# Six small tiles placed ahead of the token operands xH and xL: a shift of 224 bytes per partition

## The chip, the cores and the metric

The kernel runs on one core of a Trainium2 chip. The metric is the device time of one execution in microseconds (us); the time of a kernel is the median of its runs. One execution was also recorded by the hardware profiler, and all rows below come from that one. Each core has a matrix engine (TensorE, PE in the rows; PEld is its loading of weights), a vector engine (VectorE, DVE), a scalar engine (ScalarE, ACT), GpSimd (POOL) and a queue engine (SyncE, SP). They share a memory of 128 partitions, SBUF; an address below is a byte offset inside a partition.

## The reference: what is computed

One transformer block over 256 tokens of width 2048: an attention and recurrence mixer, and then a product-key expert layer (PEER) with 16,384 experts.

```
mod = silu(c) @ ada_w + ada_b                 # six rows of 2048: sh1, sc1, gt1, sh2, sc2, gt2
h = rms_norm(x, norm_mix_g) * (1 + sc1) + sh1
x = x + gt1 * hybrid_mixer(h, w_in, w_out, ...)     # z = h @ w_in, attention, RG-LRU, y @ w_out
h = rms_norm(x, norm_ffn_g) * (1 + sc2) + sh2
q = h @ peer_wq                               # 256 x 2048, scored against 16 sets of 128 keys
...                                           # top 16 of each half, top 16 of their sums, softmax g
act = gelu(einsum('td,thkd->thk', h, down[e])) * g
x = x + gt2 * einsum('thk,thkd->td', act, up[e])
```

The kernel computes the down product for all 16,384 experts (`h @ down.T`), multiplies by a dense table of gates that is zero for experts not picked, and multiplies by all of `up`.

## The kernel before, in words

Weights stream from HBM in tiles `raw` of 1 MB (`load`, L177), four buffers deep, on SyncE's queue. `next_part` (L273) takes half of such a tile and splits it: ScalarE rounds it to the type float32r (`wh`, L197), VectorE subtracts to get the remainder (`wl`, L198). Activations are split in the same way: `xH` and `xL` hold the 256 tokens of the current product input, 16 slices of 128 features by 256 tokens; `ah` and `al` hold the activations of the experts. Each product is then the sum of three matmuls: high by high, high by low, low by high.

There are two forms of it, and they differ in which operand is loaded into the array (stationary, 128 columns) and which is streamed through it (moving):

- `mm_sub` (L350, matmuls at L346 to L348): tokens are stationary, 128 at a time; weights move, 512 columns at a time. It is used with `xH` and `xL` for the input projection (results `f`, `a`, `r`, `xg`) and the output projection (`y`), and with `ah` and `al` for the up product (`u`).
- `mm_turn` (L356, matmuls at L363 to L365): weights are stationary, 128 columns at a time; tokens move, all 256 at once. It is used for the queries (`wq`) and the down product (`d`), both with `xH` and `xL`.

In `mm_turn` the two operands of a matmul are `wh[:, kk, ws]` (stationary) and `bH[:, kc]` (moving), where `bH` is `xH`:

```
T.matmul(o, wh[:, kk, ws], bH[:, kc], start=f and i % 2 == 0, stop=False)
T.matmul(o, wh[:, kk, ws], bL[:, kc], start=False, stop=False)
T.matmul(o, wl[:, kk, ws], bH[:, kc], start=False, stop=e and i % 2 == 1)
```

The gate logits (`gl`) use the same three products with 24 columns of weights stationary and the tokens moving.

The order of the program is: adaLN rows and the input projection (0 to 205 us), attention and recurrence with the rest of the projection between them (to 364 us), the output projection (to 474 us), the queries (to 574 us), the first 14 of 32 blocks of the down product with the building of the gate table (`w`) between their matmuls (to 930 us), and then blocks of the up product and the other blocks of the down product in turn, to the end. The order on every engine is fixed when the program is built.

Tiles of the pool `cp` live through the whole kernel and get their addresses in the order in which the code asks for them. In the built program they begin at byte 16,512 with `con`, `sm`, `row`, `cb`, `mod`, `cs` (32,512 to 32,576), then `xH`, `xL`, and then six small tiles for the decay of the recurrence (`spl`, `nsp`, `hb`, `e8`, `s8`, `q8`, 224 bytes together), which `softplus` (L417) fills at the start and `recurrence` (L734) reads.

Of the kernel before, what the change touches and what calls it, by code (L numbers as in the profile page):

```python
# [7 lines left out]
F32 = mybir.dt.float32  # L8
# [7 lines left out]
P = 128  # L16
# [8 lines left out]
RB = 8  # L25
# [40 lines left out]
def kernel(  # L66
# [26 lines left out]
    cp = ctx.enter_context(tc.tile_pool(name="cp", bufs=1))  # L93
# [19 lines left out]
    cb = cp.tile([P, D], F32, name="cb")  # L113
    mod = cp.tile([P, 6, NDC], F32, name="mod")
    cs = cp.tile([P, NDC], F32, name="cs")
    xH = cp.tile([P, NDC, S], F32R, name="xH")
    xL = cp.tile([P, NDC, S], F32R, name="xL")
    ident = con[:, C_ID:C_ID + P]
# [291 lines left out]
            yield  # L410
            A.copy(dst[:, j * 512:(j + 1) * 512], bp)

    spl = cp.tile([P, RB], F32, name="spl")
    nsp = cp.tile([P, RB], F32, name="nsp")
    hb = cp.tile([P, 2, RB], F32, name="hb")

    def softplus():  # L417
        e8 = cp.tile([P, RB], F32, name="e8")
        s8 = cp.tile([P, RB], F32, name="s8")
        q8 = cp.tile([P, RB], F32, name="q8")  # L420
        lam = sm[:, S_LAM:S_LAM + 8]
        A.activation(e8, lam, AF.Abs)
        A.activation(e8, e8, AF.Exp, scale=-1.0)
        V.tensor_scalar(s8, e8, 2.0, None, OP.add)
        V.reciprocal(s8, s8)
        V.tensor_mul(s8, s8, e8)
        V.tensor_mul(q8, s8, s8)
        V.tensor_scalar(spl, q8, 1.0 / 17, 1.0 / 15, OP.mult, OP.add)
        for kk in (13, 11, 9, 7, 5, 3, 1):
            V.tensor_mul(spl, spl, q8)  # L430
            V.tensor_scalar(spl, spl, 1.0 / kk, None, OP.add)
        V.tensor_mul(spl, spl, s8)
        V.tensor_scalar(q8, lam, -1.0, 0.0, OP.mult, OP.max)
        V.scalar_tensor_tensor(out=spl, in0=spl, scalar=2.0, in1=q8, op0=OP.mult, op1=OP.add)
        V.tensor_scalar(nsp, spl, -4.0, None, OP.mult)
        V.tensor_scalar(spl, spl, 2.0, None, OP.mult)
        V.tensor_scalar(hb, sm[:, S_BA:S_BA + 16].rearrange("p (a k) -> p a k", a=2), 0.5, None, OP.mult)
# [33 lines left out]
    for q in range(4):  # L471
        V.tensor_tensor(xt[:, 4 * q:4 * q + 4], xt[:, 4 * q:4 * q + 4], rr.unsqueeze(1).to_broadcast([P, 4, S]), OP.mult)

    softplus()

    def wide(name):
# [938 lines left out]
```

## Time and profile before

| | |
|---|---|
| median of 3 runs | 2073.27 us (2071.88 to 2073.3) |
| the profiled execution | 2070.29 us, its span 2068.5 us |
| PE busy | 1998.7 us, 97% of the span, 12602 matmuls |
| PEld busy | 1769.3 us, 86% |
| DVE busy | 1451.6 us, 70% |
| ACT busy | 1018.0 us, 49% |
| mean granted clock of TensorE | 0.987 of full speed |
| HBM traffic | 245 GB/s over the span |

Busy time of PE is the union of the times in which a matmul is in the array. Matmuls overlap: a matmul of `d` lasts 282 ns in the record, but the next one starts long before it ends. The pace of PE is therefore the distance from one start to the next, which a listing in order of time shows, and not the duration.

### The profile page before, as it was taken

The page shows a single profiled execution, that of the slowest core. Times are in us where ns is not written, and L with a number is a line of the kernel's source. Part 1 is how long each engine was busy: PE and PEld are TensorE (multiplying, and loading weights), DVE is VectorE, ACT ScalarE, POOL GpSimd, SP SyncE. Part 2 cuts the span into 40 slices and gives each one's busy share as a digit, 9 for nine tenths or more (in the row PEclk, how much of TensorE's full clock was granted, in tenths as well). Part 3 has the DMA queues.
Part 4 walks back from the last instruction along what each step waited for, and adds up shares of the span by engine and source line. Part 5 has one row for each costly group of instructions (what it writes and reads, how often), then busy time and mean ns, then how long its engine had stood idle before and what let it go on. Part 6 is the DMA issues. An engine that isn't in the chain of part 4 may idle for free.

```text
span 2068.5 us, 31265 instructions
## 1 busy us (share of the span) xinstructions
PE 1998.7 (97%) x12602; PEld 1769.3 (86%) x12602; DVE 1451.6 (70%) x2149; ACT 1018.0 (49%) x1454; POOL 61.0 (3%) x95
## 2 busy tenths in 40 slices
PE   5999997998999999999999999999999999999998
PEld 4777665778999999998888789999999999999997
DVE  7888999987999666546667766665555555555566
ACT  3445676545447887644444434444444444444442
POOL 0000000000000000001000000000000000000000
PEclk8999998998999999999999999999999999999999
DMA  9897788994555656768777877775566666565563
GB/s 374 331 371 314 265 336 319 347 344 173 174 182 185 246 207 241 278 242 296 255 242 254 285 248 259 255 262 197 194 199 207 204 203 206 195 205 201 196 223 132
DMA packets 75873, 509.12 MB, mean 246 GB/s; under 512 B 8528, under 2 KB 9040, under 8 KB 20176
## 3 DMA queue, kind: packets, MB, share of 16 engines
q1 hardware_dynamic: 63792, 450.50, 60.5%
q0 software_dynamic: 11936, 56.63, 8.2%
q8 instruction: 98, 1.61, 0.3%
q14 instruction: 47, 0.39, 0.1%
HBM read 478.78 MB, written 28.31 MB: 245 GB/s over the span
## 4 chain that ended last, share of the span: by engine, by line
PE 75%; issue 10%; DVE 9%; DMA 4%; ACT 1%; POOL 1%; DVEq 0%; SPq 0%; POOLq 0%; ACTq 0%
PE d L363 10%; PE d L365 10%; PE d L364 10%; PE u L347 7%; PE u L348 7%; PE u L346 7%; PE w L1198 3%; DVE wl L198 3%; DVE av L219 2%; DMA raw<-in_ada_w_dram 2%; PE wq L363 2%; PE wq L364 2%; PE wq L365 1%; PE a L347 1%; PE a L348 1%
## 5 line engine op out<-in xcount | busy, mean ns | idle before, releaser
L198 DVE TENSOR_TENSOR wl<-raw,wh 128x1024 fp32r<-128x1024 f32 x649 | 789.7, 1222 | 475.9 <-ACT wh L197 475.1
L197 ACT CAST wh<-raw 128x1024 fp32r<-128x1024 f32 x649 | 679.6, 1050 | 826.7 <-PE u L348 372.2
L363 PE MATMUL d<-xH,wh 128*128 128x256 f32 x2048 | 577.7, 282 | 0.0
L364 PE MATMUL d<-xL,wh 128*128 128x256 f32 x2048 | 573.0, 280 | 0.0
L365 PE MATMUL d<-xH,wl 128*128 128x256 f32 x2048 | 572.2, 279 | 0.3 <-DVE wl L198 0.3
L347 PE MATMUL u<-wl,ah 128*128 128x512 f32 x1024 | 399.4, 390 | 3.4 <-DVE wl L198 3.3
L346 PE MATMUL u<-wh,ah 128*128 128x512 f32 x1024 | 398.6, 389 | 0.0
L348 PE MATMUL u<-wh,al 128*128 128x512 f32 x1024 | 398.5, 389 | 0.0
L364 PEld LDWEIGHTS d<-xL,wh 128*128 128x128 f32 x2048 | 385.4, 188 | 0.7
L363 PEld LDWEIGHTS d<-xH,wh 128*128 128x128 f32 x2048 | 385.1, 188 | 0.7
L365 PEld LDWEIGHTS d<-xH,wl 128*128 128x128 f32 x2048 | 385.1, 188 | 0.5 <-DVE wl L198 0.5
L347 PEld LDWEIGHTS u<-wl,ah 128*128 128x128 f32 x1024 | 192.2, 188 | 44.9 <-DVE wl L198 5.9
L348 PEld LDWEIGHTS u<-wh,al 128*128 128x128 f32 x1024 | 192.3, 188 | 40.0
L346 PEld LDWEIGHTS u<-wh,ah 128*128 128x128 f32 x1024 | 192.3, 188 | 39.6
L219 DVE SCALAR_TENSOR_TENSOR av<-av,cb 128x2048 f32<-128x2048 f32 x64 | 145.9, 2285 | 5.3 <-DMA av<-in_ada_w_dram 5.3
L1182 DVE TENSOR_TENSOR oh<-con,idT 128x1024 f32<-128x1024 f32 x64 | 78.0, 1224 | 62.5 <-PE w L1198 62.5
L1203 ACT ACTIVATE oh<-oh,gT 128x128 f32<-128x128 f32 x256 | 83.3, 396 | 26.3 <-DVE oh L1182 26.1
L363 PE MATMUL wq<-xH,wh 128*128 128x256 f32 x256 | 73.2, 287 | 2.5 <-ACT xH L197 2.5
L364 PE MATMUL wq<-xL,wh 128*128 128x256 f32 x256 | 72.9, 285 | 0.0
L365 PE MATMUL wq<-xH,wl 128*128 128x256 f32 x256 | 72.5, 283 | 0.0
L1259 DVE TENSOR_TENSOR acc<-acc,u 128x512 f32<-128x512 f32 x112 | 71.6, 681 | 0.0
L1198 PE MATMUL w<-oh 128*128 128x128 f32 x512 | 69.8, 276 | 0.0
(359 smaller groups left out, 2008.3 us busy)
## 6 DMA issues: line engine op xcount, KB each, us to landing
raw<-in_down_dram SPq DMA_DIRECT2D x128, 1024.0 KB, 5.2
raw<-in_up_dram SPq DMA_DIRECT2D x128, 1024.0 KB, 5.1
av<-in_ada_w_dram SPq DMA_DIRECT2D x64, 1024.0 KB, 7.0
raw<-in_w_a_dram SPq DMA_DIRECT2D x32, 1024.0 KB, 9.1
raw<-in_ada_p_dram SPq DMA_DIRECT2D x16, 1024.0 KB, 7.3
raw<-in_w_out_dram SPq DMA_DIRECT2D x16, 1024.0 KB, 8.0
raw<-in_wq_dram SPq DMA_DIRECT2D x16, 1024.0 KB, 5.5
wd<-stg POOLq DMA_DIRECT2D x8, 2048.0 KB, 8.0
```

What stands on the lines that cost most here:

```text
L197: A.copy(dst_h, src)
L198: V.tensor_tensor(dst_l, src, dst_h.bitcast(F32), OP.subtract)
L219: V.scalar_tensor_tensor(out=t, in0=t, scalar=1.0, in1=cb, op0=OP.mult, op1=OP.mult, accum_out=m)
L346: T.matmul(o, ah, bh, start=first, stop=False)
L347: T.matmul(o, ah, bl, start=False, stop=False)
L348: T.matmul(o, al, bh, start=False, stop=last)
L363: T.matmul(o, wh[:, kk, ws], bH[:, kc], start=f and i % 2 == 0, stop=False)
L364: T.matmul(o, wh[:, kk, ws], bL[:, kc], start=False, stop=False)
L365: T.matmul(o, wl[:, kk, ws], bH[:, kc], start=False, stop=e and i % 2 == 1)
L1182: V.tensor_tensor(oh, iota.unsqueeze(1).unsqueeze(1).to_broadcast([P, 4, 2, P]), idT[:, 4 * q:4 * q + 4].unsqueeze(3).to_broadcast([P, 4, ...
L1198: T.matmul(wps[p_][:, k * P:(k + 1) * P], oh[:, k, 1], oh[:, k, 0], start=True, stop=True)
L1203: A.activation(ohs[p_][:, k, 0], ohs[p_][:, k, 0], AF.Copy, scale=gT[:, t:t + 1])
```

## The change

The six small tiles are allocated right after `cs`, ahead of `xH` and `xL`, instead of after them. They take 224 bytes, so `xH` and `xL` stand 224 bytes higher, and the small tiles 32,768 bytes lower. The pool ends at the same byte, so no other tile moves. The instructions of every engine, their order and what they wait for are the same in both programs; only addresses differ.

```diff
     mod = cp.tile([P, 6, NDC], F32, name="mod")
     cs = cp.tile([P, NDC], F32, name="cs")
+
+    spl = cp.tile([P, RB], F32, name="spl")
+    nsp = cp.tile([P, RB], F32, name="nsp")
+    hb = cp.tile([P, 2, RB], F32, name="hb")
+    e8 = cp.tile([P, RB], F32, name="e8")
+    s8 = cp.tile([P, RB], F32, name="s8")
+    q8 = cp.tile([P, RB], F32, name="q8")
     xH = cp.tile([P, NDC, S], F32R, name="xH")
     xL = cp.tile([P, NDC, S], F32R, name="xL")
...
-    spl = cp.tile([P, RB], F32, name="spl")
-    nsp = cp.tile([P, RB], F32, name="nsp")
-    hb = cp.tile([P, 2, RB], F32, name="hb")
-
     def softplus():
-        e8 = cp.tile([P, RB], F32, name="e8")
-        s8 = cp.tile([P, RB], F32, name="s8")
-        q8 = cp.tile([P, RB], F32, name="q8")
```

The addresses of the matmul operands in the two built programs. Slices of these tiles start at multiples of 512 bytes from the tile's start, so the remainders hold for every slice of 128, 256 or 512 columns:

| tile | before | after | rest by 512, before and after | rest by 64 |
|---|---|---|---|---|
| `xH` | 32,576 | 32,800 | 320, 32 | 0, 32 |
| `xL` | 48,960 | 49,184 | 320, 32 | 0, 32 |
| `wh`, `wl` (pool `wp`, 3 buffers each) | 98,336 to 118,816 | the same | 32 | 32 |
| `wh`, `wl` (pool `xp`, first stage alone) | | the same | 96 | 32 |
| `ah`, `al` (4 buffers each) | from 161,824 | the same | 32 | 32 |

Against the weights `wh` and `wl` of the pool `wp`, the token operands of the input, output, query and down products thus stand 288 bytes off (by 512) before, and 0 after. Those of the up product, `ah` and `al`, stand 0 off in both.

## Rows read from the trace of the kernel before

**Rows 1.** Busy time by stretch: us, each engine's busy us (instructions), granted clock, DMA.
```profile
core 0: us, PE busy (x) PEld busy (x) DVE busy (x) ACT busy (x) POOL busy (x), PEclk, DMA share, GB/s
0.00:205.00 205.00, 175.58 (x722) 138.55 (x723) 168.96 (x217) 92.01 (x137) 0.99 (x6) 0.95 0.89 350
205.00:364.00 159.00, 139.25 (x832) 92.27 (x830) 151.16 (x367) 105.56 (x243) 2.61 (x4) 0.95 0.79 301
364.00:474.00 110.00, 102.58 (x468) 82.34 (x468) 96.73 (x133) 53.64 (x77) 4.58 (x9) 0.95 0.90 342
474.00:574.00 100.00, 99.44 (x825) 99.04 (x825) 88.11 (x358) 48.09 (x60) 0.54 (x1) 0.97 0.49 169
574.00:930.00 356.00, 352.84 (x3005) 351.27 (x3005) 244.94 (x326) 236.92 (x461) 14.62 (x26) 1.00 0.64 226
930.00:1210.00 280.00, 277.09 (x1318) 231.68 (x1317) 198.08 (x230) 121.69 (x120) 20.26 (x28) 1.00 0.77 267
1210.00:2000.00 790.00, 789.48 (x5166) 722.76 (x5166) 460.19 (x473) 337.08 (x343) 16.32 (x20) 1.00 0.63 214
```

**Rows 2.** What PE waited for: us in total, times, longest us.
```profile
PE f L346 <- ACT xH L197: 15.4, 1, 15.4
...
PE u L347 <- DVE wl L198: 3.3, 4, 1.6
...
PE d L365 <- DVE wl L198: 0.3, 1, 0.3
```

**Rows 3.** Groups by line: form, count, busy us, mean ns, idle before.
```profile
L363 PE MATMUL d<-xH,wh 128*128 128x256 f32 x2048 | 577.7, 282 | 0.0
...
L363 PEld LDWEIGHTS d<-xH,wh 128*128 128x128 f32 x2048 | 385.1, 188 | 0.7
...
L363 PE MATMUL wq<-xH,wh 128*128 128x256 f32 x256 | 73.2, 287 | 2.5 <-ACT xH L197 2.5
...
L346 PE MATMUL y<-wh,xH 128*128 128x512 f32 x128 | 51.7, 406 | 3.6 <-ACT xH L197 3.6
...
L346 PE MATMUL a<-wh,xH 128*128 128x512 f32 x128 | 49.3, 397 | 1.8 <-ACT wh L197 1.8
...
L346 PE MATMUL f<-wh,xH 128*128 128x512 f32 x96 | 37.9, 415 | 15.4 <-ACT xH L197 15.4
...
L346 PE MATMUL xg<-wh,xH 128*128 128x512 f32 x32 | 13.5, 428 | 0.0
...
L346 PE MATMUL r<-wh,xH 128*128 128x512 f32 x32 | 12.9, 413 | 1.7 <-ACT wh L197 1.7
```

**Rows 4.** PE in order of time, a block of `d`: start us, us, what.
```profile
1221.34 0.28 PE L363 MATMUL d<-xH,wh 128*128 128x256 f32 x1
...
1243.74 0.39 PE L346 MATMUL u<-wh,ah 128*128 128x512 f32 x1
```

**Rows 5.** PE in order of time, the output projection.
```profile
437.83 0.40 PE L347 MATMUL y<-wl,xH 128*128 128x512 f32 x1
...
442.50 0.40 PE L346 MATMUL y<-wh,xH 128*128 128x512 f32 x1
```

**Rows 6.** PE in order of time, a block of the up product.
```profile
1289.99 0.39 PE L346 MATMUL u<-wh,ah 128*128 128x512 f32 x1
...
1299.96 0.39 PE L348 MATMUL u<-wh,al 128*128 128x512 f32 x1
```

**Rows 7.** PE in order of time, the gate logits.
```profile
262.77 0.28 PE L346 MATMUL gl<-xH,wh 128*24 128x256 f32 x1
...
264.36 0.28 PE L348 MATMUL gl<-xH,wl 128*24 128x256 f32 x1
```

**Rows 8.** Weight loads in order of time, merged: 8 loads before matmuls of one column.
```profile
354.88 0.97 PEld L879 LDWEIGHTS nha<-con,sqa 128*128 128x128 f32 x8
```

**Rows 9.** Groups by line: the casts that write `wh` and `xH`, and the subtractions.
```profile
L197 ACT CAST wh<-raw 128x1024 fp32r<-128x1024 f32 x648 | 679.1, 1051 | 826.7 <-PE u L348 372.2 <-PE d L364 297.3 <-PE y L348 44.2
...
L197 ACT CAST xH<-x1T 128x512 fp32r<-128x512 f32 x8 | 4.6, 615 | 0.8 <-DVE x1T L1060 0.7
```

## The prediction

> **What bounds the kernel now.** I read the busy times by stretch first, then what PE waited for, then the pace of its matmuls in the listing in order of time. In the stretches from 574 us on PE is busy 352.8 of 356, 277.1 of 280 and 789.5 of 790 us, at full clock; VectorE has 58 to 71% and the DMA engines 63 to 77% [rows 1]. The listed waits of PE for VectorE come to 3.3 us in `u` and 0.3 us in `d` [rows 2]. So from the queries (474 us) on, the end is set by how fast one matmul follows another, and the other engines have room. Before 474 us it is different: the DMA engines are busy 79 to 90% of the time and VectorE 82 to 95%, with PE at 86 to 93% [rows 1]. There, a faster matmul would mostly wait.
>
> The reader should then look at paces, not durations. A block of `d` has 192 matmuls (8 steps, 2 slices, 4 column groups, 3 products); the first starts at 1221.34 us and the first matmul behind the block at 1243.74 [rows 4]. That is 22.40 / 192 = 116.7 ns for 256 columns. Counted at one column per cycle of the full 2.4 GHz, 256 columns would take 106.7 ns, so 10.0 ns are lost, or 0.039 ns per column. In `y`, 20 matmuls lie between 437.83 and 442.50 [rows 5]: 233.5 ns for 512 columns, which need 213.3; 20 ns are lost, again 0.039 per column. In `u`, 44 matmuls lie between 1289.99 and 1299.96 [rows 6]: 226.6 ns, 13.3 lost, 0.026 per column.
>
> `y` and `u` run the same form: the same moving tiles `wh` and `wl`, 512 columns, stationary tiles of 128 by 128. What differs is the stationary tile: `xH` and `xL` at a remainder of 320 (by 512), 288 away from that of the weights, against `ah` and `al`, which have the weights' own remainder of 32. `d` has the roles exchanged, the same distance of 288, and the same loss per column as `y`. The gate logits move the same `xH` with only 24 columns of weights to load: 14 matmuls between 262.77 and 264.36 [rows 7], 113.6 ns for 256 columns, 0.027 per column. So moving `xH` itself can go at the better pace, and it is in company with a full weight load at another remainder that it goes at the worse one.
>
> **The change part by part.** It adds and removes no instruction, wait or DMA. Three things move.
>
> The small tiles (32 or 64 bytes per partition) get other addresses. They are read as scalars and filled once; I take 0.
>
> Writes to `xH` and `xL` land at another remainder. A cast of 512 columns into `xH` takes 615 ns at the old place, and one of 1024 columns into `wh`, which already has the new remainder, 1051 ns [rows 9]. Half of the latter is less than the former, and a start-up time explains it, so I take 0. If the whole difference, 2 x 615 - 1051 = 179 ns, came from the remainder, the 24 casts would give back at most 4 us, in stages that PE alone does not bound.
>
> The matmuls that read `xH` and `xL` get both operands at the same remainder. Their number: `d` has 3 x 2048 = 6144 and `wq` 3 x 256 = 768 [rows 3], 6912 together, in stretches that PE bounds. `y` has 3 x 128, `a` 3 x 128, `f` 3 x 96, `xg` and `r` 3 x 32 each: 1248, all before 474 us.
>
> No row has a moving operand of 256 float32r columns at remainder 32 beside a full weight load at 32. The nearest are `u` (all remainders 32, but 512 columns) and `gl` (256 columns moving, but a short load). Both lose 0.026 to 0.027 ns per column. With 0.026, `d` comes to 106.7 + 6.7 = 113.4 ns, 3.3 ns less than now. A floor lies just below: loads of 128 columns of weights that nothing else slows follow each other at 0.111 us (8 loads in 0.97 us, of which one, 188 ns, is the last one's own length [rows 3, 8]: (970 - 188) / 7). So the most that `d` could gain is 116.7 - 111.7 = 5.0 ns, and the least is nothing or a loss (below). I take 3.3, since `u` and `gl` agree from two sides: 6912 x 3.3 = 22.8 us.
>
> For `y` and its like the analogue is complete (`u`, all operands then at the same remainders): 233.5 - 226.6 = 6.9 ns, 1248 x 6.9 = 8.6 us if all of it counted. In their stretches DMA and VectorE stand close behind, so I count a third, 3 us; the bounds are 0 and 8.6.
>
> What takes over when PE goes faster: at 3% more pace VectorE rises from 88 to 91% in the queries, and from 69 to 71% in the first blocks of `d`; nothing becomes the bound there.
>
> The sum on the profiled execution's own time is 2070.3 - 22.8 - 3 = 2044.5 us. It lies 3.0 us under the median of the runs, so I forecast 2073.3 - 25.8 = 2047.5, and give 2047.
>
> One rule speaks against all this. Row for row, `y` and `u` differ by 6.9 ns with the same moving tile [rows 5, 6], and nothing but the stationary tile's place differs. The Trainium skill ("SBUF — State Buffer", section "Who interferes with whom") says that PE has two independent read ports, one for the moving operand and one for the weight load, and never waits on anyone. By that rule no address could matter and the sum would be 0, a time of 2073. The trace does not agree with it as far as `y` is concerned, unless another cause stands behind those 6.9 ns; that is the first rival.
>
> **The rivals.** *No effect.* `y` could be slow for a reason that the change leaves as it is: that `xH` lies low in the partition (32 to 65 KB) and `ah` at 161 KB or more, or that the projection stages have more DMA traffic (0.79 to 0.90 against 0.63 [rows 1]). Against traffic: the pace in `u` hardly varies, and `d` at 0.63 loses as much per column as `y`. Against the place: `d` moves `xH` slowly and `gl` moves the same `xH` fast. Time: 2073, give or take 4. The Trainium skill's rule on the ports, cited above, would put it here. Chance 0.12.
>
> *The stationary operand's own remainder is what counts.* Then `xH` at a multiple of 64 was bad as a stationary operand, only `y` and its like gain, and `d`, whose weights stay where they are, keeps its 116.7 ns. Time: 2073.3 less 0 to 8.6, about 2070 at the third counted above. For it: it fits `y` against `u`. Against it: the equal loss per column in `d` would be chance. Chance 0.08.
>
> *The loss goes with the weight load, and grows when both streams start at the same place.* This is the other side. A load lasts about as long as 256 columns move, so in `u` all 13.3 ns could arise while the load runs, and in `d` 13.3 ns over 256 columns would then make 106.7 + 13.3 = 120.0 ns, 3.3 more than now: 6912 x 3.3 = 22.8 us more, less the 3 us of `y`, 2093. It decides from the point where the pace of `d` rises over 117 ns. The same comes out if a moving operand that is not on a multiple of 64 costs something: today `xH` in `d` is on one, and after the change it is not. For it: `u` and `y` both move an operand off a multiple of 64, so no row shows what that costs by itself. Against it: `gl` loses 6.9 ns with a load of 24 columns, less than a fifth of a full load, so the loss does not shrink with the load. Chance 0.14.
>
> *The change does what I say, as far as the floor:* `d` at 111.7 and all of `y`, 2073.3 - 34.6 - 8.6 = 2030. I count it as the low end of my forecast, with 2035 as a sensible bound, since the floor and all of `y` at once are unlikely.
>
> **How the numbers follow.** My forecast (equal remainders give the pace of `u` and `gl`) has 0.66. Its own range is 2035 to 2055: the upper end is a pace of 114.0 ns in `d`, 6912 x 2.7 = 18.7 us, and nothing from `y`. A measurement of this kernel can tell about 0.2%, 4 us, from no change. Faster by more than that: the forecast and half of the second rival, 0.70. Within it: the first rival and the other half, 0.16. Slower: 0.14. To leave no more than 2 in 10 out, the range takes in the first two rivals, 2035 to 2076, and leaves out the third.
>
> **What would show it.** Right: the 192 matmuls of a block of `d` take 21.8 us in place of 22.4, the pace of `y` is that of `u`, 227 ns, `u` is unchanged, and the stretch from 574 us on is some 20 us shorter. The step on `d` is wrong if its pace stays 116 to 117 while `y` falls to 227 (then the stationary side alone counts), or rises to 118 or more (then the weight load's overlap or the alignment to 64 does). The step on `y` is wrong if it keeps 233. If both paces fall and the time does not, the gain went into waits for `wl`, which would then show as PE waiting for VectorE or DMA in `d`.

## The result, and the profile after

The changed kernel takes 2088.25 us (median of 4 runs, 2086.84 to 2091.13) against 2073.28 us in the same comparison: a ratio of 1.0072, with a 95% interval of 1.0054 to 1.0089. It is slower by 15 us, where 26 us less was forecast. The third rival of the prediction, at 2093 us, was close. Two of the eight runs of the kernel with only `xL` moved, below, were slow, at 2497 and 5313 us, and stand in none of its numbers.

The busy times by stretch of the changed kernel, to be held against [rows 1] (instructions in brackets):

```profile
core 0: us, PE busy (x) PEld busy (x) DVE busy (x) ACT busy (x) POOL busy (x), PEclk, DMA share, GB/s
364.00:474.00 110.00, 100.30 (x469) 81.77 (x469) 97.65 (x135) 54.94 (x78) 5.42 (x10) 0.95 0.90 344
474.00:574.00 100.00, 100.00 (x821) 99.61 (x822) 87.39 (x356) 46.90 (x58) 0.54 (x1) 0.98 0.49 169
...
1210.00:2000.00 790.00, 789.71 (x5059) 721.99 (x5058) 454.64 (x466) 332.06 (x336) 16.32 (x20) 1.00 0.62 212
```

PE is as busy as before from 1210 to 2000 us, 789.7 of 790, at the same granted clock. But it gets through 5059 matmuls in that time, and before through 5166. The loss is inside the stream of matmuls, where a busy share can't show it. What PE waited for, beside [rows 2]:

```profile
PE f L353 <- ACT xH L204: 16.8, 2, 15.4
...
PE u L354 <- DVE wl L205: 5.3, 5, 2.2
```

The waits changed by a few us in total, and in `d` none is listed. So the paces remain. PE in order of time in the changed kernel: a block of `d`, 20 matmuls of `y`, 44 of `u` (start us, us, what), against [rows 4 to 6]:

```profile
437.80 0.39 PE L355 MATMUL y<-wh,xL 128*128 128x512 f32 x1
...
442.33 0.39 PE L354 MATMUL y<-wl,xH 128*128 128x512 f32 x1
...
1227.61 0.28 PE L370 MATMUL d<-xH,wh 128*128 128x256 f32 x1
...
1250.64 0.40 PE L353 MATMUL u<-wh,ah 128*128 128x512 f32 x1
...
1254.75 0.39 PE L353 MATMUL u<-wh,ah 128*128 128x512 f32 x1
...
1264.72 0.39 PE L355 MATMUL u<-wh,al 128*128 128x512 f32 x1
```

The 192 matmuls of `d` take 23.03 us, 120.0 ns each, where they took 116.7. `y` takes (442.33 - 437.80) / 20 = 226.5 ns, where it took 233.5. `u` keeps 226.6. So `y` did what was forecast and `d` the opposite.

Where the time went, from the matmuls' first and last starts, by tile (duration min/median/max, then the starts). Before:

```profile
L363 PE MATMUL wq<-xH,wh x256: 277/281/582, 474.6 to 572.5; 128*128 128x256 f32 x128
...
L363 PE MATMUL d<-xH,wh x2048: 274/280/367, 574.0 to 1996.6; 128*128 128x256 f32 x187
...
L346 PE MATMUL u<-wh,ah x1024: 387/389/397, 954.9 to 2061.6; 128*128 128x512 f32 x171
```

After:

```profile
L370 PE MATMUL wq<-xH,wh x256: 281/283/582, 473.9 to 573.0; 128*128 128x256 f32 x128
...
L370 PE MATMUL d<-xH,wh x2048: 277/283/366, 574.4 to 2014.3; 128*128 128x256 f32 x187
...
L353 PE MATMUL u<-wh,ah x1024: 387/389/397, 958.9 to 2079.3; 128*128 128x512 f32 x171
```

Up to the queries 0.7 us are gained (474.6 to 473.9). All that reached the end here from the faster `y`, `a` and `f` is in these 0.7 us, and they are no more than the spread of that moment: later runs with the distances of before came to the queries at 474.9 and 476.9 us, and later ones with those of after at 475.4 and 473.8. The queries lose 1.1 us of it again (the first `d` is 0.4 us late), and from the first to the last `d` 17.3 us are lost. The span of the profiled execution grew by 17.7 us, from 2068.5 to 2086.2.

Of the 17.3, the first 14 blocks of `d`, up to the first `u`, make 3.6 (380.9 to 384.5 us). The blocks of `u` behind them, up to the block of `d` shown above, make 2.3 (266.4 to 268.7); there the listed waits of `u` for `wl` grew by 2.0, from 3.3 to 5.3 us. Whether the change makes these waits is not shown: with the same distances, the run at 0 with the short matmuls (below) took 267.2 us for that stretch. The 18 blocks that alternate with the up product make 11.4, and 18 x 192 x 3.28 ns = 11.3. At 3.3 ns for each matmul the first 14 blocks would have lost 8.9. They lost less because much of them had not run at 116.7 ns before: their last 815 matmuls had run at 117.8 (see "History" below).

### The profile page after: what moved, and what is told of

It reads as the page before. It is cut to its first block, busy times and chain, and to the rows that moved or that the text cites. A ratio compares the mean times of both kernels' runs of the same rounds, so it can differ in the third digit from the quotient of the medians.

```text
span 2086.2 us, 31265 instructions
## 1 busy us (share of the span) xinstructions
PE 2012.1 (96%) x12602; PEld 1785.9 (86%) x12602; DVE 1451.1 (70%) x2149; ACT 1017.6 (49%) x1454; POOL 61.0 (3%) x95
## 4 chain that ended last, share of the span: by engine, by line
PE 74%; DVE 10%; issue 9%; DMA 4%; ACT 2%; POOL 0%; SPq 0%; DVEq 0%; POOLq 0%; ACTq 0%
PE d L371 11%; PE d L372 11%; PE d L370 11%; PE u L354 7%; PE u L355 7%; PE u L353 7%; DVE wl L205 3%; DVE av L226 3%; PE w L1198 3%; DMA raw<-in_ada_w_dram 2%; PE wq L370 2%; PE wq L371 2%; PE wq L372 1%; PE y L355 1%; PE y L353 1%
## 5 line engine op out<-in xcount | busy, mean ns | idle before, releaser
L370 PE MATMUL d<-xH,wh 128*128 128x256 f32 x2048 | 584.0, 285 | 0.0
L371 PE MATMUL d<-xL,wh 128*128 128x256 f32 x2048 | 580.5, 283 | 0.0
L372 PE MATMUL d<-xH,wl 128*128 128x256 f32 x2048 | 580.5, 283 | 0.0
L371 PEld LDWEIGHTS d<-xL,wh 128*128 128x128 f32 x2048 | 393.0, 192 | 0.7
L370 PEld LDWEIGHTS d<-xH,wh 128*128 128x128 f32 x2048 | 392.8, 192 | 0.7
L372 PEld LDWEIGHTS d<-xH,wl 128*128 128x128 f32 x2048 | 392.7, 192 | 0.0
```

## The experiments

"Distance" below is the start of the loaded operand (weights in `d`) less the start of the moved one, by 512 bytes: 224 in `d` before, 0 after. All paces are times between starts of matmuls in the listing in order of time; a time of a kernel without a spread is that of a single run.

**Only xL moved.** The six tiles stand between the two operands; nothing is added.

```diff
     xH = cp.tile([P, NDC, S], F32R, name="xH")
+    spl = cp.tile([P, RB], F32, name="spl")
...
+    q8 = cp.tile([P, RB], F32, name="q8")
     xL = cp.tile([P, NDC, S], F32R, name="xL")
```

> The six small tiles stand between xH and xL: xH is where it was before (288 off the weights, on a multiple of 64), xL is where the change puts it (0 off, 32 past a multiple of 64). Distance theory (the loss belongs to one matmul and the weight load that runs beside it, by the distance of their addresses): of the three matmuls in d only the one that moves xL goes to 120.0 ns, the two that move xH keep 116.7, and the time is about a third of the way, 2073 + 6912/3 x 3.3 ns = 2081, less up to 2 us from y. A theory of one common pace (all three slow down when one does, or the small tiles' own place is the cause) expects all three at 120, or all at 116.7. It does not tell distance from alignment to 64.

2076.74 us (median of six runs, 2075.62 to 2079.62), a ratio of 1.0022 (1.0010 to 1.0034): about a third of the way, as the distance theory had it. A block of `d`:

```profile
1223.68 0.28 PE L369 MATMUL d<-xH,wh 128*128 128x256 f32 x1
...
1246.30 0.40 PE L352 MATMUL u<-wh,ah 128*128 128x512 f32 x1
```

That is 22.62 / 192 = 117.8 ns, a third of the way from 116.7 to 120.0. But the loss does not sit in the one matmul. In the 18 blocks the pace, from a matmul's start to the next, was 117.8 ns for the matmuls that move `xH` and 117.8 for the one that moves `xL`, where 116.7 and 120.0 were expected. Neighbours share it.

**Everything moved by 32 bytes.** The order of before, and an unused tile ahead of all.

```diff
+    pad32 = cp.tile([P, 8], F32, name="pad32")
     con = cp.tile([P, C_END], F32, name="con")
```

> The order of before, with 32 unused bytes ahead of everything: xH, xL, the weights, ah and al all move by 32 bytes, so the distances stay (288 and 0), while xH and xL leave the multiples of 64 and the weights, ah and al come onto them. Distance theory: every pace as before, d 116.7, y 233.4, u 226.7 ns, time 2073. Alignment theory (a moving operand that starts off a multiple of 64 costs): d goes to 120, y and u, whose moving weights now start on a multiple of 64, get faster than 233 and 227; time 2073 + 23 - 20 or less.

2070.93 us in one run beside 2072.92 for the kernel before. A block of `d` and 22 matmuls of `y` in it:

```profile
436.72 0.40 PE L354 MATMUL y<-wl,xH 128*128 128x512 f32 x1
...
441.86 0.40 PE L355 MATMUL y<-wh,xL 128*128 128x512 f32 x1
...
1221.98 0.28 PE L370 MATMUL d<-xH,wh 128*128 128x256 f32 x1
...
1244.38 0.39 PE L353 MATMUL u<-wh,ah 128*128 128x512 f32 x1
```

22.40 / 192 = 116.7 ns and 5.14 / 22 = 233.6 ns, as before, although every operand changed its place against the multiples of 64. The half of the third rival that blamed a moving operand off a multiple of 64 has fallen, and so has, for a shift of 32 bytes, an effect of the addresses as such. What is left is how the two operands stand to each other.

**Other distances.** In each run the small tiles are only dealt out anew ahead of, between and behind `xH` and `xL`; in the first two `ah` and `al` were shifted as well, by unused tiles behind `acc` and between `ah` and `al`. The edit of the first:

```diff
+    hb = cp.tile([P, 2, RB], F32, name="hb")
...
+    q8 = cp.tile([P, RB], F32, name="q8")
     xH = cp.tile([P, NDC, S], F32R, name="xH")
+    spl = cp.tile([P, RB], F32, name="spl")
     xL = cp.tile([P, NDC, S], F32R, name="xL")
+    nsp = cp.tile([P, RB], F32, name="nsp")
...
         h = pool.tile([P, 4, S], F32R, tag="ah", bufs=4, name=f"ah{eb}")
+        if eb == 0:
+            pool.tile([P, 120], F32, name="padL")
...
             acc = upp.tile([P, NT, D], F32, name="acc")
+            upp.tile([P, 16], F32, name="padA")
```

> Other distances, weights less token operand by 512: 64 for xH, 32 for xL; ah and al less the weights 64 and 32. Distance theory: paces that have not been seen yet, between 112 ns (loads alone) and 121 for d, and different for the matmuls of xH and xL; from the gate logits, which are slow (118 ns) at 64, 160 and 192 and fast (113) at 0, 32, 96, 128 and 224, xH should be worse than xL. Alignment theory: 120 for xH (32 past a multiple of 64), 116.7 for xL (on one); u unchanged at 226.7, since its moving weights stay.

2104.21 us. In the 18 blocks of `d` 117.3 ns for the matmuls that move `xH` (64) and 122.0 for `xL` (32), the reverse of what the gate logits suggested, and the reverse of the alignment theory. A block of `u`, 96 matmuls, with the start behind it:

```profile
1253.57 0.39 PE L352 MATMUL u<-wh,ah 128*128 128x512 f32 x1
...
1276.15 0.28 PE L369 MATMUL d<-xH,wh 128*128 128x256 f32 x1
```

22.58 / 96 = 235.2 ns. Over all of `u` the mean went from 226.9 to 235.3, which alone makes 3072 x 8.4 = 26 us. How it splits between `ah` and `al` depends on the counting: 236.8 (64) and 232.5 (32) by the time before a matmul's own start, in which its tokens are loaded, but 234.4 and 237.3 by the time behind it.

> Distances 128 for xH and 96 for xL; ah and al less the weights 128 and 96. Distance theory: again paces of their own between 112 and 121 ns in d, and others than 226.7 in u. Alignment theory: as in s1, 120 for xH and 116.7 for xL, u at 226.7.

2092.77 us. `d` at 117.5 (128) and 118.5 (96), `u` at 233.3 on average. The moving tiles of `u` had not been touched in these two runs: a shift of the loaded operand alone costs time too. These two runs change two things at once, so only their paces are used, and not their times.

> xH and xL both stand 192 off (weights less token operand, by 512; before 224, after 0); nothing else differs. Distance theory with the loss in the stretch of the weight load: a pace of its own in d, the same for all three matmuls; the gate logits were slow at 192 and fast at 224, so more than before: 117 to 121 ns, time 2074 to 2100. Alignment theory, already contradicted: 120, as all tokens are 32 past a multiple of 64. The up product keeps 226.7.

2079.37 us: `d` at 117.8, `wq` at 117.8.

> Both 160 off, tokens on a multiple of 64. Distance theory: again a pace of its own, by the gate logits slow (117 to 121 ns). Alignment theory: 116.7 ns, time 2073.

2090.27 us: `d` at 120.0, `wq` at 119.9, with the tokens on a multiple of 64, where the alignment theory had 116.7. A block of `d`, 192 matmuls in 23.05 us:

```profile
1228.76 0.28 PE L369 MATMUL d<-xH,wh 128*128 128x256 f32 x1
...
1251.81 0.39 PE L352 MATMUL u<-wh,ah 128*128 128x512 f32 x1
```

> Both 64 off. With xL at 32 the mixed case gave 117 to 123 ns over the three matmuls. Distance theory: one pace for all three, 117 to 121. If neighbours with other distances had made the mixed case slow, it comes out nearer to 117.

2071.76 us, and two paces with the same addresses. The block of `d` at 1532 us, and the one before it, in which four transposes of `bcast_row` (`bc`) stand behind its second matmul:

```profile
1487.96 0.28 PE L370 MATMUL d<-xL,wh 128*128 128x256 f32 x1
1488.32 0.65 PE L414 MATMUL bc<-con,mod 128*128 128x128 f32 x4
1488.72 0.37 PE L371 MATMUL d<-xH,wl 128*128 128x256 f32 x1
...
1510.36 0.39 PE L352 MATMUL u<-wh,ah 128*128 128x512 f32 x1
...
1532.13 0.28 PE L369 MATMUL d<-xH,wh 128*128 128x256 f32 x1
...
1554.75 0.39 PE L352 MATMUL u<-wh,ah 128*128 128x512 f32 x1
```

190 matmuls in 21.64 us, 113.9 ns, with the first of them slowed by the interruption; and 192 in 22.62 us, 117.8 ns. Seventeen of the 18 blocks behind the up product ran at 117.8, this one and the queries (113.4 to 113.9 ns over their four blocks, without the interruptions) at about 113.4. So the distance does not fix the pace alone. The expectation of one pace was wrong.

**The cost by itself.** In the code ahead of the queries, trains of equal matmuls that load and move slices of `xH` and feed nothing. They ran from 481.5 to 793 us, at a granted clock of 1.00, with the DMA engines busy 2% and VectorE 5.3 us of that time.

```diff
     fill(AHEAD)
+    flat = xH.rearrange("p k t -> p (k t)")
+    scratch = ps_p("scratch")
+
+    def train(n, w, off, count):
+        for _ in range(count):
+            T.matmul(scratch[0:w, 0:n], flat[:, 2048 + off:2048 + off + w], flat[:, 0:n], start=True, stop=True)
+
+    for off in range(0, 128):
+        train(256, P, off, 12)
+    for off in range(0, 128, 4):
+        train(512, P, off, 10)
+    for w in (96, 64, 32):
+        for off in range(0, 128, 8):
+            train(256, w, off, 10)
```

> The changed kernel with 2336 extra matmuls ahead of the queries that feed nothing: in trains of 10 or 12 the same slices of xH are loaded and moved, with the distance (loaded less moved, by 512 bytes) going from 0 to 508 in steps of 4 for 256 columns moved and 128 loaded, in steps of 16 for 512 columns moved, and in steps of 32 for loads of 96, 64 and 32 columns. Distance theory with the loss in the stretch of the load: 120.0 ns at 0 and 116.7 at 224 for 256 columns, 226.7 at 0 and 233.4 at 224 and 288 for 512, so at 0 the same 13.3 ns for both, and at other distances other values, in a pattern; narrower loads lose less at the same distance. A theory by which the loss goes with the moved columns (as the prediction had it) expects at each distance twice the loss for 512 columns that 256 have, whatever the load. If the place in memory, other engines or the difference of the tiles counted, the trains would all have one pace.

Mean pace of a train in ns, from its third start to its last, at the distances that are multiples of 32. Where a distance and the same plus 256 came out differently, the second stands behind the stroke:

```
distance                0            32           64           96           128          160          192          224
256 moved, 128 loaded   119.3/119.8  118.8/118.7  113.3        117.4        118.6        119.7        113.3        116.8
512 moved, 128 loaded   230.3/226.6  233.6        233.0        234.3        233.9/234.0  233.1/233.0  229.0        233.1
256 moved,  96 loaded   116.6/115.6  116.4/118.0  117.9/118.0  116.7/117.7  118.6        118.4/117.9  117.7/113.3  116.4/116.7
256 moved,  64 loaded   113.3        116.7        118.4        117.1        116.6        118.1/118.3  120.0        118.6
256 moved,  32 loaded   113.3/113.7  117.4/117.6  113.9/113.7  113.3/113.4  113.4/113.3  117.6        113.3/113.4  117.0/116.9
```

Four of these trains as the listing in order of time merges them (start us, us from the first start to the last end, count): 256 columns at 0 and at 64, 512 columns at 224 and at 256.

```profile
481.98 0.88 PE L1277 MATMUL scratch<-xH 128*128 128x256 f32 x6
...
504.42 0.96 PE L1277 MATMUL scratch<-xH 128*128 128x256 f32 x7
...
695.40 1.79 PE L1277 MATMUL scratch<-xH 128*128 128x512 f32 x7
...
700.67 1.52 PE L1277 MATMUL scratch<-xH 128*128 128x512 f32 x6
```

A matmul of 256 columns lasts 0.28 us and one of 512 lasts 0.39, so the paces are (0.88 - 0.28) / 5 = 0.120, (0.96 - 0.28) / 6 = 0.113, (1.79 - 0.39) / 6 = 0.233 and (1.52 - 0.39) / 5 = 0.226 us. (The third takes in the last start of the train before it.) With one engine and one tile, and hardly anything else running, the trains give the paces of `d` before (116.8 at 224), of `d` after (120.0 at 0, once it is steady), of `y` before (233.6 at 288, in the table at 32) and of `u` (226.6). For the same columns they differ in the distance alone. Only the loaded operand moves from train to train, and only the moved operand was shifted in the runs of `d`; at 0 (once steady), at 160 and, in the 18 blocks, at 224 both give the same pace to within 0.3 ns. So it is the distance, and not the place of either operand.

Three things are to be seen. With 128 columns loaded the pattern repeats by 256 bytes: all 128 distances in steps of 4 bytes, of which the table shows 16, gave the same at 256 more, to within 0.1 ns but for 0 with its unsteady start. No train is faster than 113.3 ns for 256 columns, or 226.6 for 512: 0.026 ns per column over the 106.7 and 213.3 of the prediction is the floor of what was seen. And at 0, 512 columns are on the floor and 256 columns are 6.7 ns above it; at 64 it is the other way, 19.7 above 213.3 against 6.6 above 106.7. With 64 or fewer columns loaded the extra at 0 is gone.

The theory that the loss goes with the moved columns has fallen: at 64 the ratio is 3 and at 0 it is 1. The other one, a fixed loss for each load, holds at 0 and fails at 64 as well. That narrower loads lose less holds at 0, but not at 64 or 192: there a matmul with 64 columns loaded takes longer (118.4 and 120.0 ns) than one with 128 (113.3).

**History.** The layouts at 64, at 0 and at 224, with one short matmul ahead of each of the 18 blocks of `d`.

```diff
-    def mm_turn(pst, kcs, wh, wl, first, last, bH, bL):
+    def mm_turn(pst, kcs, wh, wl, first, last, bH, bL, lead=0):
+        if lead and first:
+            T.matmul(pst[0][:, 0:lead], wh[:, 0, 0:P], bH[:, kcs[0], 0:lead], start=True, stop=True)
...
-                    add(ev_d(eb, turned(f"d{eb}")), 0)
+                    add(ev_d(eb, turned(f"d{eb}", lead=64)), 0)
```

> The layout at 64 off, and one more matmul ahead of each of the 18 blocks of d that alternate with the up product: the block's first matmul with 64 of its 256 columns, whose result the full one replaces. In the run at 64 off without it, all blocks of wq and one block of d that began after PE had waited ran at 113.4 ns, the blocks that came straight behind the up product at 117.7, with the same addresses. History theory (where distance allows two paces, the start of the load against the moving decides, and it holds until something breaks it): the short matmul, shorter than a load, makes PE wait once and the blocks go to 113.4 ns; 18 x 192 x 4.2 ns = 14.7 us less and 18 x 0.11 = 2 us more than the run without it, about 2059. If the distance alone sets the pace, and the fast blocks had another cause, 117.7 stays and the time is 2074.

2060.09 us in six runs (2057.61 to 2061.46), a ratio to the kernel before of 0.9934 (0.9920 to 0.9948), 13 us faster than it. The start of a block and the first matmul behind it:

```profile
1528.17 0.19 PE L365 MATMUL d<-xH,wh 128*128 128x64 f32 x1
1528.18 0.19 PEld L371 LDWEIGHTS d<-xH,wh 128*128 128x128 f32 x1
1528.20 0.36 PE L371 MATMUL d<-xH,wh 128*128 128x256 f32 x1
1528.29 0.19 PEld L372 LDWEIGHTS d<-xL,wh 128*128 128x128 f32 x1
1528.41 0.28 PE L372 MATMUL d<-xL,wh 128*128 128x256 f32 x1
...
1550.07 0.39 PE L352 MATMUL u<-wh,ah 128*128 128x512 f32 x1
```

The short matmul gives way after 0.03 us, the next takes 0.21 us to its follower, whose weight load begins only at 1528.29, 0.11 us behind the load before it, and from there 191 matmuls run to 1550.07 at (1550.07 - 1528.41) / 191 = 113.4 ns. Nothing but the start differs from the blocks at 117.8. So at 64 the start of a block decides between the two paces.

> The changed kernel (0 off) with the same short matmul ahead of the 18 blocks. If 0 has one pace alone, as all its blocks of wq and d show, d stays at 120.0 ns and the time at 2088 plus 2. If the history decides here too, these blocks go to 113 to 117 and the time falls by 10 to 23 us.

2090.78 us. After its short start a block of `d` here:

```profile
1228.56 0.28 PE L372 MATMUL d<-xL,wh 128*128 128x256 f32 x1
...
1251.47 0.40 PE L352 MATMUL u<-wh,ah 128*128 128x512 f32 x1
```

22.91 / 191 = 119.9 ns. The same disturbance changes nothing at 0.

> The kernel before (224 by the measure of weights less tokens) with the same short matmul. If 224 has one pace alone, d stays at 116.7 ns and the time is 2073 plus 2; if the history decides here too, the blocks move to another pace, 113 to 120.

2073.97 us, the 18 blocks of `d` at 116.7 ns behind the short start. The disturbance changes nothing at 224 either. Yet 224 does not have one pace alone. In the kernel before, two stretches of the queries, each of 167 matmuls without an interruption:

```profile
507.50 0.28 PE L364 MATMUL wq<-xL,wh 128*128 128x256 f32 x1
...
526.87 0.28 PE L365 MATMUL wq<-xH,wl 128*128 128x256 f32 x1
...
531.69 0.28 PE L364 MATMUL wq<-xL,wh 128*128 128x256 f32 x1
...
551.24 0.28 PE L365 MATMUL wq<-xH,wl 128*128 128x256 f32 x1
```

(526.87 - 507.50) / 166 = 116.7 ns and (551.24 - 531.69) / 166 = 117.8 ns, with the same addresses. In the run with the short matmuls, whose queries are the same, all four such stretches went at 116.7. The last 815 matmuls of the first 14 blocks of `d` went at 117.8 in both. In the run with everything moved by 32 bytes one stretch of 116 matmuls went at 120.0. At 0 no second pace was seen: every stretch of 40 or more matmuls of `wq` and `d` in the changed kernel went at 120.0.

## Why the prediction was wrong, point by point

**What bounds the kernel** was right: from 474 us on, the pace of matmuls sets the end, and the other engines had room. A change of 3.3 ns in `d` went to the end whole in the last stretch: 11.4 us measured, 11.3 by the pace.

**That it matters how the two operands stand to each other** was right, and is shown by the run with everything moved by 32 bytes, by the runs at other distances and by the trains. The rival "no effect" has fallen. The rule named beside it, in the Trainium skill ("SBUF — State Buffer", section "Who interferes with whom": PE's read ports for the moving operand and for the weight load are independent, and PE never waits on anyone), would have all the trains alike; they ran from 113.3 to 122.3 ns with 256 columns moved and 128 loaded. The rival of the loaded operand's own remainder has fallen too: the weights of `d` stayed where they were, and its pace went from 116.7 to 120.0.

**The step that failed** is the price of `d` at equal remainders: "I take 3.3, since `u` and `gl` agree from two sides". 22.8 us of gain were counted, and the term measured 16.1 us of loss (1.1 in the queries, 3.6 in the first 14 blocks of `d`, 11.4 in the 18 others): 120.0 ns at equal remainders, where 113.4 were expected. Both neighbours were read wrongly. `u` showed that 512 columns lose nothing above the floor at 0, and I carried its 0.026 ns per column over to 256 columns, for which no row had both operands at one remainder; at 0 they pay 6.7 ns more. `gl` has a short load, and it stands at no single distance: its 16 slices of 24 columns begin 96 bytes apart in `wh` and `wl`, so that they run through all 16 multiples of 32 by 512, before as after. I took its mean for the price of moving `xH` with any load. The equal loss per column in `d` and `y` at 224 and 288, 0.039 ns, on which the per-column view rested, is a coincidence of two different patterns. And 116.7 ns, read from one block, was not the pace of all 6912 matmuls: parts of the queries and of the first 14 blocks ran at 117.8.

**The third rival** had the pace of 120.0 ns to the tenth and 2093 us, 5 too many, mostly because it priced the queries and the first 14 blocks at 3.3 ns for each matmul as well: 11.4 us for 3456 matmuls, where 4.7 were lost. That the tenth fits is in part luck, as its reasons show. Its first reason, a loss of 13.3 ns for each full load at 0 whatever moves, agrees with the trains at 0, but is no law: it fails at 64. Its second reason, the alignment to 64, is contradicted. My argument against it from `gl` was the wrong reading named above.

**The term of `y`** had its mechanism right, 226.5 ns in place of 233.5, and the size too large: the queries began 0.7 us earlier, which is within the spread of later runs, where 3 were counted between bounds of 0 and 8.6. The analogue was not complete for all 1248 matmuls either: 240 of `a` and `f` read weights from the pool `xp`, at a remainder of 96, and went from a distance of 224 to 448, where the trains have 233.1 and 229.0 ns. The stretches before 474 us have VectorE and DMA close behind PE, as [rows 1] said.

**The small tiles and the writes** cost nothing that a row shows, as counted. The waits of `u`, which were counted at nothing, grew by 2.0 us, as said above.

What stays open is what inside the engine makes the pattern. The runs show that it depends on the distance by 256 bytes, on the columns loaded and moved, and on what went before. How the stream began decided at 64; what decides at 224, where two paces and once a third were seen, is open. At 192 the trains ran at 113.3 ns and the kernel at 117.8, so that distance may have two paces as well; the block of `d` that other matmuls interrupt stayed at 117.8 there, and a short start was not tried. Where a stream mixes two distances the trains do not give its pace: `u` at 64 and 32 took 235.3 ns on average, the trains 233.0 and 233.6.

## What to carry to other kernels

Where PE is busy all the time, look at the distance between starts of matmuls before looking for idle time: the same instruction may go at 113 or 120 ns, and busy shares hide it. Where operands are loaded and moved from the same memory, where they stand to each other is a parameter like a tile size, and it is measured with trains of matmuls in the form that the kernel uses (columns loaded and moved), not inferred from another form. An analogy that is complete but for one dimension (here 512 against 256 columns) is not a bound, and the pace of one block is not that of all: take several stretches of the trace.

## What the runs showed of the hardware that was not expected

- The start of the loaded operand less that of the moved one changes the pace of float32r matmuls at the full clock: 113.3 to 122.3 ns with 256 columns moved and 128 loaded, 226.6 to 234.3 ns with 512 moved. With 128 columns loaded the pattern repeats by 256 bytes.
- At one distance two paces can hold. At 64, blocks of 192 matmuls ran at 117.8 ns throughout or, behind a short matmul, at 113.4 ns throughout. At 224, stretches of the queries ran at 116.7 or at 117.8 ns in one and the same execution.
- The best distances are not the same for the two sizes: 0 is among the best seen for 512 columns (226.6, once steady) and one of the worse for 256 (120.0), 64 gives 233.0 and 113.3.
